# A decoder trunk with expert retrieval: one background chain split into two paced chains, with own weight rings, kept queries, eleven row tiles and a shared last sum

## The chip, the cores and the metric

The program runs on one core of one Trainium2 chip. The metric is device time in microseconds (us) of one execution; a smaller number is better. Engines are named as the profile names them: PE (matrix multiply), PEld (its weight loads), DVE (vector), ACT (activation), POOL (here it issues the gathers) and SP (here it issues the other DMAs). Each works through its own instructions in the order in which they stand.

## The reference, cut to what matters

A sequence of 272 tokens (16 meta tokens and 256 inputs, 1024 wide, float32) passes two layers. Layer 0 is a Conformer convolution, layer 1 a differential attention with 8 heads. After each comes a retrieval of experts:

```
def chunk(xc):                                   # 128 tokens at a time
    q = (xc @ wq).reshape(PEER_CHUNK, PEER_HEADS, 2, PEER_HALF)
    s1 = jnp.einsum('chd,kd->chk', q[:, :, 0], sk1)
    s2 = jnp.einsum('chd,kd->chk', q[:, :, 1], sk2)
    v1, i1 = lax.top_k(s1, PEER_TOPK)
    v2, i2 = lax.top_k(s2, PEER_TOPK)
    ...                                          # best 16 of the 256 sums v1 + v2
    expert = jnp.take_along_axis(cand_i, top_pos, axis=-1)
    gate = jax.nn.softmax(top_s.astype(jnp.float32), axis=-1).astype(xc.dtype)
    u = u_tab[expert]
    v = v_tab[expert]
    act = jax.nn.gelu(jnp.einsum('cd,chkd->chk', xc, u), approximate=False)
    return jnp.einsum('chk,chkd->cd', gate * act, v)
```

Each token reads 8 heads x 16 experts in each layer, and one expert is 1024 + 1024 floats (u and v side by side, 8 KB). A last rmsnorm gives the output, 256 x 1024.

## The kernel before, in words

**Row tiles and phases.** One gather (`Group.fetch`, L647) brings, for one head and one of its 16 choices, the expert of each of 128 tokens: a tile `row` of 128 x 2048 floats, 1 MB. I call this a row tile; there are 528, numbered from 0. They come in five phases (layer, token block): (0,0) is row tiles 0 to 127, the meta tokens (0,2) 128 to 143, (0,1) 144 to 271, (1,0) 272 to 399 and (1,1) 400 to 527. Each head of a phase is 16 row tiles in a row.

**What is done with one.** DVE multiplies its u half with the token vectors and sums (`product`, L653). For two row tiles together ACT takes the gelu (`gelu`, L658) and DVE multiplies by the gates (`weigh`, L662). For each row tile ACT then builds a diagonal matrix (L679) and PE adds the weighted v half to the sums in PSUM (`add`, L681: two matmuls, each of which the trace counts as two instructions). The row tile's buffer is free after that add. There are `NR = 10` buffers, so POOL can issue a gather only when the add ten row tiles earlier is done.

**The front.** Before the first gather stand the convolution and the choice of the first head. PE multiplies 16 blocks of `pw1` in three passes (`mm24`, L190); after block 0 stands the rmsnorm of the input (`stat`, L223, and `spread_rows`, L233).

**The background.** All other work is one generator, `background()`: the rest of the convolution, the choice of experts for layer 0, attention of token block 0, choice of (1,0), attention of block 1, choice of (1,1). The loop over row tiles pulls `RATE` units (0.3 to 1.2) of it for each row tile. The choice for one head is two queries (`query`, 8 matmuls L239 each), their scores (`ranked`, L555) with `top16` on DVE (L454 to L458), and `candidates`, `resolve` and `gates` (L508 to L539). For heads 2 to 7 of layer 0 one query serves both token blocks (272 columns), and both blocks are chosen at once (`for i in range(n)` in `ranked`). The recording layer then orders the instructions of each engine anew by its own estimates, so the program text is not the order on an engine.

**Weights.** Every 512 KB block of `fwq`, `wkvq` and `wo` passes through one ring of `NW = 5` buffers, in the one order of need, issued by SP (L165).

**The end.** After the last `add`, `final(1)` squares both halves on ACT (L863), takes the inverse root (`rsqrt`, with an ACT table load at L199), multiplies on DVE (L870) and writes two halves out from SP (L872).

## Time and profile before

| what | value |
|---|---|
| median of 3 runs | 1667.83 us (1666.53 to 1667.98) |
| the profiled execution | 1667.95 us |
| its span, first to last instruction | 1666.2 us |
| around the span | 1.75 us |
| read from HBM over the span | 627.51 MB, 377 GB/s |
| mean granted PE clock | 0.976 |

The profiled execution stands 0.12 us from the median. Busy times of the engines overlap and do not add up; a stage is read by what ends last in it.

### The profile page before, as it was taken

To read this page: it belongs to the slowest core of one execution; us is meant where nothing else is said; L and a number is where in the kernel's file an instruction comes from. 1 tells how busy PE (TensorE), PEld (TensorE's weight loads), DVE (VectorE), ACT (ScalarE), POOL (GpSimd) and SP (SyncE) were. 2 spreads that over 40 slices of the span, in tenths; PEclk is the share of its full clock that TensorE was granted. 3 is DMA by queue.
4 is the path that set the end of the run, shared out by engine and by line. 5 is a ranking of instruction groups with operands and counts; after the bars stand their busy time and mean duration, and the time that the engine had idled before them with its cause. 6 is when DMAs were issued, how large, how long until landed. Compare 5 with 4: busy or idle time off the path is not lost.

```text
span 1666.2 us, 18716 instructions
## 1 busy us (share of the span) xinstructions
PE 1441.8 (87%) x5560; PEld 828.2 (50%) x5560; DVE 1126.5 (68%) x3331; ACT 612.4 (37%) x1602; POOL 502.4 (30%) x533
## 2 busy tenths in 40 slices
PE   7998989988778799999888889999988787777776
PEld 7998745553222356656553356666553332223222
DVE  6984689998555465656996566666997555555554
ACT  8725434444112343453433254353342231121122
POOL 0001323333333323233224323232324343333330
PEclk9998999998999899999999999999999999999999
DMA  7301999998999999999999999999999999999996
GB/s 287 129 2 62 420 414 389 372 386 330 421 421 422 421 419 415 418 405 418 418 419 417 421 416 416 418 418 418 419 413 353 421 422 420 422 422 421 422 421 251
DMA packets 98388, 629.80 MB, mean 378 GB/s; under 512 B 11248, under 2 KB 11888, under 8 KB 30704
## 3 DMA queue, kind: packets, MB, share of 16 engines
q0 software_dynamic: 76032, 553.68, 80.8%
q1 hardware_dynamic: 22256, 74.92, 11.5%
q8 instruction: 46, 0.75, 0.2%
q14 instruction: 54, 0.44, 0.1%
HBM read 627.51 MB, written 1.05 MB: 377 GB/s over the span
## 4 chain that ended last, share of the span: by engine, by line
PE 35%; DMA 31%; DVE 29%; ACT 2%; issue 2%; POOL 0%; DVEq 0%; SPq 0%; POOLq 0%; ACTq 0%
DMA row<-in_fuv,eidx 29%; PE acc L681 21%; DVE row L653 10%; PE mm L239 7%; DVE vcc L394 3%; DVE scr L456 2%; PE mm L307 2%; DMA row<-in_fuv,meidx 1%; DVE oh L525 1%; DVE oh L528 1%; DVE ev L530 1%; DVE idxu L455 1%; DVE idxu L458 1%; DVE lo L143 1%; DVE pu L455 1%
## 5 line engine op out<-in xcount | busy, mean ns | idle before, releaser
L681 PE MATMUL acc<-row,dg 128*128 128x512 f32 x2048 | 963.1, 612 | 172.5 <-ACT dg L679 172.2
L647 POOL DMA_INDIRECT row<-in_fuv,eidx x512 | 485.4, 948 | 1107.3 <-PE acc L681 591.9
L653 DVE SCALAR_TENSOR_TENSOR row<-row,xps 128x1024 f32<-128x1024 f32 x528 | 639.8, 1215 | 249.3 <-DMA row<-in_fuv,eidx 233.4
L681 PEld LDWEIGHTS acc<-row,dg 128*128 128x128 f32 x2048 | 374.0, 193 | 640.5 <-issue 360.3
L658 ACT ACTIVATE dot<-dot,stf 128x2 f32<-128x2 f32 x256 | 75.6, 295 | 626.5 <-DVE row L653 626.1
L679 ACT ACTIVATE dg<-cst,dot 128x128 f32<-128x128 f32 x512 | 179.0, 394 | 157.7 <-DVE dot L662 148.4
L239 PEld LDWEIGHTS mm<-xin,w 128*128 128x128 f32 x1472 | 196.3, 194 | 39.2 <-issue 31.1
L239 PE MATMUL mm<-xin,w 128*128 128x128 f32 (+2 forms) x1472 | 214.2, 297 | 0.0
L662 DVE TENSOR_TENSOR dot<-dot,gate 128x2 f32<-128x2 f32 x256 | 40.8, 159 | 77.1 <-ACT dot L658 77.0
L658 ACT ACT_TABLE_LOAD x59 | 75.7, 1283 | 1.0
L394 DVE SCALAR_TENSOR_TENSOR vcc<-u,dw,vcc 128x272 f32<-128x272 f32 (+2 forms) x176 | 64.9, 412 | 0.6
L653 DVE DVE_READ_ACCUMULATOR row<-row,xps 128x1 f32 x528 | 43.3, 82 | 0.0
L537 ACT ACT_TABLE_LOAD x33 | 42.3, 1283 | 0.6
L714 DVE LOAD_MASK_SELECT rt<-mm x32 | 0.4, 14 | 56.0 <-PE mm L239 56.0
L555 PE MATMUL mm<-sk,qsb 128*128 128x128 f32 x120 | 24.3, 299 | 13.2 <-ACT qsb L547 13.2
L681 PE MATMUL acc<-row,mg 128*16 128x512 f32 x64 | 28.7, 593 | 7.6 <-ACT mg L675 7.6
L454 DVE MAX8 vals<-mm 128x8 f32<-128x128 f32 x64 | 18.5, 290 | 24.0 <-PE mm L555 23.8
L239 PEld LDWEIGHTS mm<-osb,w 128*128 128x128 f32 x256 | 30.9, 192 | 6.8 <-issue 5.5
L555 PEld LDWEIGHTS mm<-sk,qsb 128*128 128x128 f32 x120 | 18.7, 189 | 30.2 <-ACT qsb L547 21.2
L383 PE MATMUL acc<-u,dg 128*128 128x272 f32 x140 | 32.9, 392 | 0.0
L547 ACT ACTIVATE qsb<-mm 128x128 f32<-128x128 f32 (+2 forms) x48 | 14.6, 303 | 45.4 <-PE mm L239 44.9
L190 PE MATMUL mm<-xh,hi 128*128 128x272 f32 x128 | 24.8, 315 | 7.4 <-ACT hi L142 5.8
(222 smaller groups left out, 1226.5 us busy)
## 6 DMA issues: line engine op xcount, KB each, us to landing
w<-in_fwq SPq DMA_DIRECT2D x48, 512.0 KB, 8.4
w<-in_wkvq SPq DMA_DIRECT2D x48, 512.0 KB, 8.0
row<-in_fuv,eidx POOLq DMA_INDIRECT x512, 15.7
w<-in_wo SPq DMA_DIRECT2D x16, 512.0 KB, 8.7
raw<-in_pw SPq DMA_DIRECT2D x15, 512.0 KB, 4.0
row<-in_pw SPq DMA_DIRECT2D x8, 512.0 KB, 8.3
hT<-in_h SPq DMA_DIRECT2D x4, 272.0 KB, 5.0
out_dram<-row SPq DMA_DIRECT2D x4, 256.0 KB, 2.1
```

Source lines behind the costliest of these rows:

```text
L239: PE.matmul(out, lhsT=w[:, j, :], rhs=x[:, j, c0:c0 + n], start=(j == 0), stop=(j == ND - 1))
L307: PE.matmul(acc[:, :n], lhsT=pw2[b][:, d, :], rhs=cc[:, d, c0:c0 + n], start=(d == 0 and not part), stop=(d == ND - 1))
L394: V.scalar_tensor_tensor(out=y, in0=x, scalar=dw[:, i, k:k + 1], in1=y, op0=ALU.mult, op1=ALU.add)
L455: V.max_index(out=idx[:, 0:8], in_max=vals[:, 0:8], in_values=src)
L537: S.activation(g, g, AF.Exp, scale=rts, accum_out=sm)
L555: PE.matmul(sc[:, i * P:(i + 1) * P], lhsT=q[:, i * P:(i + 1) * P], rhs=sk[:, layer, half, :], start=True, stop=True)
L647: GP.indirect_dma_start(out=r, out_offset=None, in_=a["fuv%d" % self.layer], in_offset=bass.IndirectOffsetOnAxis(ap=self.e[:, k:k + 1], ax ...
L653: V.scalar_tensor_tensor(out=u, in0=u, scalar=1.0, in1=self.ph.xps, op0=ALU.mult, op1=ALU.mult, accum_out=self.dot[:, k:k + 1])
L658: S.activation(d, d, AF.Gelu, scale=self.ph.rt)
L662: V.tensor_tensor(out=d, in0=d, in1=self.g[:, k:k + SUB], op=ALU.mult)
L679: S.activation(g, ident, AF.Copy, scale=w)
L681: PE.matmul(out[half], lhsT=g, rhs=r[:, half * 512:(half + 1) * 512], start=first, stop=last, skip_group_check=self.layer == 1)
```

## The change

The one background generator becomes two: `selection()` (all choices of experts) and `attending()` (both attentions and the first output), each pulled at its own constant pace in all phases: `SELECT` is 1.0 units for each of the first 32 row tiles and 0.55 after them, `ATTEND` 0.68. Each has its own weight ring: `wq` with 5 buffers and `wa` with 3, both still issued by SP. For layer 0 a query of 272 columns now chooses token block 0 alone; the columns of block 1 are kept in `qlate` (12 buffers) and chosen later by `choose_late`. The input of layer 1's choice gets its own buffer `xnext`. There are 11 row tiles instead of 10; the buffer `sg` moves into free columns of `vcc` for it. In the front, the rmsnorm of the input stands after block 1 of `pw1` instead of block 0. At the end the last two row tiles are taken one by one, the last one's second half is added by DVE (L703) instead of PE, and `close()` shares the last norm among ACT and DVE and writes the halves from SP and ACT.

```
-NR = 10
-NW = 5
+NR = 11
+NQ = 5
+NA = 3
-RATE = {(0, 0): 1.15, (0, 1): 1.1, (1, 0): 1.2, (1, 1): 0.3}
+SELECT = (1.0, 0.55)
+ATTEND = 0.68
...
-    weights = Weights([a["fwq"][0, j] for j in range(16)] + per_half + per_half)
+    queries = Weights("wq", NQ, [a["fwq"][l, j] for l in (0, 1, 1) for j in range(16)])
+    shared = Weights("wa", NA, ([a["wkvq"][j] for j in range(24)] + [a["wo"][j] for j in range(8)]) * 2)
...
-            cb(b, acc)
+            if b:
+                if b == 1:
+                    cb(0, before)
+                cb(b, acc)
+            before = acc
...
-            q = wk.tile([P, T], F32, name="qsb")[:, 0:n]
-            S.activation(q, acc[:, :n], AF.Copy)
+            q = wk.tile([P, P], F32, name="qsb")
+            S.activation(q, acc[:, off:off + P], AF.Copy)
+            if n == T:
+                late[h, half] = wk.tile([P, P], F32, name="qlate", bufs=12)
+                S.activation(late[h, half], acc[:, M + P:T], AF.Copy)
...
+        def choose_late(h):
+            vals = wk.tile([P, 1, 2, M], F32, name="vals")
+            idxu = wk.tile([P, 1, 2, M], U32, name="idxu")
+            for half in range(2):
+                yield from ranked(0, half, late.pop((h, half)), 1, vals, idxu)
+            yield from picked(0, h, [1], vals, idxu, rts0)
...
+                closing = (self.layer, self.t, self.h) == (1, 1, 7)
+                if closing and last:
+                    preload(AF.Sqrt)
+                    y = wk.tile([P, 512], F32, name="qhalf", bufs=1)
+                    V.scalar_tensor_tensor(out=y, in0=r[:, 512:1024], scalar=w, in1=out[1], op0=ALU.mult, op1=ALU.add)
+                    box["half"] = y
...
+        def close():
+            src = [phases[1, 1].acc[0], box["half"]]
+            gr = [box["grow"][:, k * 512:(k + 1) * 512] for k in range(2)]
+            ss = wk.tile([P, 2], F32, name="fss", bufs=1)
+            z = rp.tile([P, 2 * D], F32, name="row")
+            V.scalar_tensor_tensor(out=z[:, D:D + 512], in0=src[1], scalar=1.0, in1=src[1], op0=ALU.mult,
+                                   op1=ALU.mult, accum_out=ss[:, 1:2])
+            S.activation(z[:, D + 512:], src[0], AF.Square, accum_out=ss[:, 0:1])
+            V.tensor_tensor(out=z[:, 512:1024], in0=src[1], in1=gr[1], op=ALU.mult)
+            s1 = wk.tile([P, 1], F32, name="fs1", bufs=1)
+            V.tensor_tensor(out=s1, in0=ss[:, 0:1], in1=ss[:, 1:2], op=ALU.add)
+            r = rsqrt(wk, s1, 1, 1.0 / D, tag="f",
+                      meanwhile=lambda: V.tensor_tensor(out=z[:, 0:512], in0=src[0], in1=gr[0], op=ALU.mult))
+            V.tensor_scalar(out=z[:, 512:1024], in0=z[:, 512:1024], scalar1=r, scalar2=None, op0=ALU.mult)
+            S.activation(z[:, 0:512], z[:, 0:512], AF.Copy, scale=r)
+            for k in range(2):
+                (SY, S)[k].dma_start(out=out_ap[P:2 * P, k * 512:(k + 1) * 512], in_=z[:, k * 512:(k + 1) * 512])
...
+            yield from early(2)
+            yield from choose_late(0)
+            yield from early(3)
+            yield from early(4)
+            yield from choose_late(1)
+            yield from early(5)
+            yield from early(6)
+            yield from early(7)
...
+            yield from choose_meta()
+            for h in range(2, 8):
+                yield from choose_late(h)
+            for t in range(2):
+                yield from until(t)
+                yield from ready_layer1(t)
...
+                select.run(SELECT[0] if s < 2 * M else SELECT[1])
+                attend.run(ATTEND)
```

What the change does to the order on an engine is shown at three places. The first is PE in phase (0,0), near row tile 30: `xin,w` and `xin,wq` are queries of both token blocks, `sk,qsb` scores of a kept query, `row,dg` the adds. Before:

```order
L681 MATMUL acc<-row,dg 128x512 x8
L239 MATMUL mm<-xin,w 128x272 x5
L555 MATMUL mm<-sk,qsb 128x128 x2
L239 MATMUL mm<-xin,w 128x272 x4
L681 MATMUL acc<-row,dg 128x512 x4
L239 MATMUL mm<-xin,w 128x272 x4
L555 MATMUL mm<-sk,qsb 128x128 x2
```

And in the changed kernel:

```order
L241 MATMUL mm<-xin,wq 128x272 x5
L565 MATMUL mm<-sk,qsb 128x128
L241 MATMUL mm<-xin,wq 128x272
L707 MATMUL acc<-row,dg 128x512 x4
L241 MATMUL mm<-xin,wq 128x272 x4
L707 MATMUL acc<-row,dg 128x512 x4
```

Behind each query now stands one block's scores instead of two, and the next query follows sooner: the twelve queries of heads 2 to 7 stand between the adds of row tiles 13 and 52, before between 11 and 60.

The second place is SP in the front, where `raw` are blocks of `pw1` and `w`, `wq`, `wa` ring blocks. Before, from the loads of `pw2` (`row<-in_pw`) on:

```order
L420 DMA row<-in_pw 128x1024 x8
L135 DMA raw<-in_pw 128x1024 x3
L469 DMA sk<-in_sk 128x256 x2
L165 DMA w<-in_fwq 128x1024
L476 DMA mask<-in_cst 128x128
L477 DMA rope<-in_cst 128x544
```

In the changed kernel:

```order
L427 DMA row<-in_pw 128x1024 x8
L137 DMA raw<-in_pw 128x1024 x3
L167 DMA wq<-in_fwq 128x1024
L167 DMA wa<-in_wkvq 128x1024
L137 DMA raw<-in_pw 128x1024 x2
L167 DMA wa<-in_wkvq 128x1024 x2
L137 DMA raw<-in_pw 128x1024 x3
```

Three attention blocks now load in the front; before, the first of them stood behind eleven more `fwq` blocks that wait for buffers.

The third place is the end of DVE, after the weighing of the last row tiles. Before:

```order
L662 TENSOR_TENSOR dot<-dot,gate 128x2
L865 TENSOR_TENSOR fs_10194<-fss 128x1
L198 TENSOR_SCALAR rs_vf<-fs_10194 128x1
L202 RECIPROCAL rs_rf<-rs_sf 128x1
L203 TENSOR_TENSOR rs_sf<-rs_rf 128x1
L204 SCALAR_TENSOR_TENSOR rs_sf<-rs_sf,rs_vf 128x1
L205 SCALAR_TENSOR_TENSOR rs_rf<-rs_sf,rs_rf 128x1
L870 SCALAR_TENSOR_TENSOR row<-acc,rs_rf,zk 128x512 x2
```

In the changed kernel:

```order
L681 TENSOR_TENSOR dot<-dot,gate 128x1
L703 SCALAR_TENSOR_TENSOR qhalf<-row,dot,acc 128x512
L905 SCALAR_TENSOR_TENSOR row,fss<-qhalf 128x512
L908 TENSOR_TENSOR row<-qhalf,zk 128x512
L910 TENSOR_TENSOR fs_10239<-fss 128x1
L912 TENSOR_TENSOR row<-acc,zk 128x512
L198 TENSOR_SCALAR rs_vf<-fs_10239 128x1
L204 RECIPROCAL rs_rf<-rs_sf 128x1
L205 TENSOR_TENSOR rs_sf<-rs_rf 128x1
L206 SCALAR_TENSOR_TENSOR rs_sf<-rs_sf,rs_vf 128x1
L207 SCALAR_TENSOR_TENSOR rs_rf<-rs_sf,rs_rf 128x1
L913 TENSOR_SCALAR row<-row,rs_rf 128x512
```

Four wide instructions moved in ahead of the root, and one multiplication by it (L913) remains behind it.

## Rows read from the trace of the kernel before

**Rows 1.** The page: 40 equal slices of the span, DMA share and rate.

```profile
DMA  7301999998999999999999999999999999999996
GB/s 287 129 2 62 420 414 389 372 386 330 421 421 422 421 419 415 418 405 418 418 419 417 421 416 416 418 418 418 419 413 353 421 422 420 422 422 421 422 421 251
```

**Rows 2.** Windows by stage: length, each engine busy (instructions), PE clock, DMA share, GB/s.

```profile
0.00:158.00 158.00, 143.42 (x974) 135.49 (x974) 124.41 (x390) 94.62 (x239) 2.01 (x5) 0.96 0.31 110
158.00:240.00 82.00, 76.67 (x372) 53.99 (x373) 54.56 (x189) 35.30 (x92) 28.25 (x30) 0.94 0.99 407
240.00:410.00 170.00, 155.26 (x467) 83.67 (x466) 163.75 (x626) 75.42 (x165) 55.50 (x58) 0.96 0.95 369
410.00:1240.00 830.00, 745.48 (x3030) 425.30 (x3029) 551.02 (x1647) 310.97 (x837) 267.68 (x283) 0.99 1.01 418
1240.00:1290.00 50.00, 42.93 (x111) 19.81 (x110) 38.46 (x104) 16.43 (x40) 20.21 (x22) 0.93 0.92 360
1290.00:1640.00 350.00, 263.49 (x580) 104.47 (x579) 184.12 (x358) 73.80 (x218) 128.73 (x138) 0.99 1.01 421
1640.00:1666.00 26.00, 14.54 (x32) 5.49 (x31) 10.15 (x23) 5.90 (x15) 0.00 (x0) 0.91 0.37 151
```

**Rows 3.** Waits of POOL between 240 and 410 us: total us, times, longest.

```profile
POOL row L647 <- PE acc L681: 67.3, 28, 7.0
```

**Rows 4.** DVE's products (L653) alone in stretches; each row tile counts two instructions.

```profile
205.00:329.60 124.60, 45.93 (x76) 0.97 0.99 394
329.60:394.25 64.65, 24.28 (x40) 0.90 0.90 350
1156.58:1259.10 102.52, 38.93 (x64) 1.00 1.00 405
```

**Rows 5.** All engines, 240.3 to 394.25 us, columns as in Rows 2.

```profile
240.30:394.25 153.95, 139.21 (x430) 76.40 (x430) 150.17 (x597) 69.40 (x150) 47.65 (x49) 0.95 0.94 370
```

**Rows 6.** DVE by line, 240.3 to 394.2 us: count, busy, mean ns, idle before.

```profile
L653 DVE SCALAR_TENSOR_TENSOR row<-row,xps 128x1024 f32<-128x1024 f32 x48 | 57.7, 1203 | 0.0
...
L530 DVE TENSOR_REDUCE ev<-oh 128x32 f32<-128x512 f32 x13 | 8.8, 673 | 0.0
```

**Rows 7.** Chain that ended last, 183 to 220 us: start, us, what.

```profile
206.95 3.67 PE mm L239 x16
...
212.33 0.45 PE mm L555 x4
212.78 3.44 PE acc L681 x8
```

**Rows 8.** All engines in block 1's attention, columns as in Rows 2.

```profile
1002.00:1127.00 125.00, 125.00 (x632) 81.43 (x631) 80.06 (x239) 58.38 (x163) 37.93 (x40) 1.00 1.02 417
```

**Rows 9.** The page's DMA issues: KB each, median us to landing.

```profile
w<-in_wo SPq DMA_DIRECT2D x16, 512.0 KB, 8.7
```

**Rows 10.** The same by tile w: landing, shortest, median, longest.

```profile
DMA to landing us min/median/max: 4.5/8.2/14.3
```

**Rows 11.** Timeline of PE, 12 to 19 us: start, us, what, idle before.

```profile
13.92 2.06 PE L223 MATMUL mm<-one,sa 128*128 128x1 f32 x18
18.32 1.12 PE L233 MATMUL mm<-cst,stc 16*128 16x16 f32 x3 [2.33 <-DVE stc L227]
```

**Rows 12.** Timeline of the end, columns as in Rows 11.

```profile
1652.33 1.22 DVE L653 SCALAR_TENSOR_TENSOR row<-row,xps 128x1024 f32<-128x1024 f32 x1 [1.25 <-DMA row<-in_fuv,eidx]
...
1657.51 0.60 ACT L863 ACTIVATE row<-acc 128x512 f32<-128x512 f32 x1 [2.64 <-PE acc L681]
...
1659.07 1.28 ACT L199 ACT_TABLE_LOAD   x1
...
1660.37 0.20 ACT L199 ACTIVATE rs_sf<-rs_vf 128x1 f32<-128x1 f32 x1
...
1661.46 1.41 DVE L870 SCALAR_TENSOR_TENSOR row<-acc,rs_rf,zk 128x512 f32<-128x512 f32 x2
1662.24 0.99 SPq L872 DMA_DIRECT2D out_dram<-row  x2
```

More of the change, by code (lines that the diff above doesn't have):

```diff
@@ L201, in rsqrt @@
             preload(then)
+        if meanwhile is not None:
+            meanwhile()
         V.reciprocal(out=r, in_=s)
@@ L421, in conv @@
                     pw2.append(w)
-                for _ in range(NW - 1):
-                    weights.fetch()
+                for _ in range(NQ - 1):
+                    queries.fetch()
         for i in range(ND - LAG, ND):
@@ L679, in add @@
                     S.activation(g, ident, AF.Copy, scale=w)
-                for half in range(2):
-                    PE.matmul(out[half], lhsT=g, rhs=r[:, half * 512:(half + 1) * 512], start=first, stop=last,
+                closing = (self.layer, self.t, self.h) == (1, 1, 7)
[4 more added lines that the diff above has]
+                    box["half"] = y
+                for half in range(1 if closing and last else 2):
+                    stop = last or (closing and half == 1 and k == M - 2)
+                    PE.matmul(out[half], lhsT=g, rhs=r[:, half * 512:(half + 1) * 512], start=first, stop=stop,
                               skip_group_check=self.layer == 1)
@@ L774, in attention @@
                 acc = bank()
-                mm8(acc[:, :P], weights.get(), xb, 0, P)
+                mm8(acc[:, :P], shared.get(), xb, 0, P)
                 qT = wk.tile([P, P], F32, name="qT")
@@ L797, in attention @@
                 yield
-                w = weights.get()
+                w = shared.get()
                 acc = bank()
@@ L851, in ready_layer1 @@
             ph.src = (xq, 0)
-            yield
             for h in range(8):
-                yield from choose(1, h, xq, n, [t], 0, [ph.rt])
+                yield from choose(1, h, xq, n, t, 0, [ph.rt])
         def final(t):
             c0, n = cols(t)
-            src = phases[1, t].acc if t else [phases[1, t].row[:, k * 512:(k + 1) * 512] for k in range(2)]
+            src = [phases[1, t].row[:, k * 512:(k + 1) * 512] for k in range(2)]
             ss = wk.tile([P, 2], F32, name="fss", bufs=1)
@@ L889, in trunk @@
         xa = xq0[:, :, 0:n]
-        first = [[weights.get(), weights.get()] for _ in range(2)]
+        first = [[queries.get(), queries.get()] for _ in range(2)]
         fill = box["fill"]
@@ L896, in trunk @@
                 next(ln)
-        one = choose(0, 0, xa, n, [0], M, rts0, first[0])
+        one = choose(0, 0, xa, n, 0, M, rts0, first[0])
         for _ in range(5):
@@ L907, in trunk, with until, selection @@
             pass
-        def background():
+        attended = {}
+        def until(t):
+            while t not in attended:
+                yield True
+        def selection():
             for b, _ in enumerate(point(1, lambda b: gain(1, b))):
@@ L912, in background @@
                     yield
-            yield from choose(0, 1, xa, n, [0], M, rts0, first[1])
+            yield from choose(0, 1, xa, n, 0, M, rts0, first[1])
             take(1)
@@ L961, in background, with __init__, run @@
             yield from final(0)
+        class Paced:
+            def __init__(self, units):
+                self.units, self.credit, self.left = units, 0.0, True
+            def run(self, rate):
+                self.credit += rate
+                while self.left and self.credit >= 1.0:
+                    self.credit -= 1.0
+                    said = next(self.units, 0)
+                    self.left = said != 0
+                    if said:
+                        self.credit = 0.0
+        select, attend = Paced(selection()), Paced(attending())
         order = [(0, 0, h) for h in range(8)]
-        bg = background()
         order.insert(META_AT, (0, 2, 0))
         order += [(l, t, h) for l, t in ((0, 1), (1, 0), (1, 1)) for h in range(8)]
-        credit, left, slots = 0.0, True, []
+        slots = []
         total = M * len(order)
@@ L973, in trunk @@
                     while key not in chosen:
-                        assert not next(bg), key
+                        if next(select.units):
+                            assert not next(attend.units), key
                     cur = Group(*key)
@@ L995, in trunk @@
                 g.add(k)
-            if s % SUB == SUB - 1 and s < total:
+            if s % SUB == SUB - 1 and s < total - SUB:
                 cur.gelu(s % M - SUB + 1)
-        for _ in bg:
-            pass
-        for _ in final(1):
-            pass
+        assert not next(select.units, 0) and not next(attend.units, 0)
+        close()
         st.close()
```

87 lines of the change are left out of this document (35 added, 52 removed).

## Prediction

> **What bounds the kernel now.** I read the page's forty slices first [rows 1]: from the fifth slice on the DMA rate stands at 413 to 422 GB/s almost everywhere, and the places where it does not are few. So I cut the span into stages at those places [rows 2]. The best long stage, 1290 to 1640 us, moves 421 GB/s for 350 us; I take that as the rate of a full DMA. At it a row tile (1.0486 MB) costs 2.49 us and a weight block (0.5243 MB) 1.245 us, and the 629.8 MB of the whole execution (627.5 read from HBM, 1.05 written, the rest instructions) 1496 us. What remains of the 1666.2 us, 170 us, is time in which DMA is not full. Stage by stage it is length x (421 - rate) / 421: 116.7 us before the first gathers, 2.7 to 240 us, **21.0** from 240 to 410, **5.9** from 410 to 1240, **7.2** from 1240 to 1290, none to 1640, and 16.7 at the end. The change leaves the bytes alone (112 weight blocks and 528 row tiles before and after), so every microsecond must come out of one of these gaps.
>
> Why is DMA not full from 240 to 410 us? POOL's longest wait there is 67.3 us in 28 waits for an add on PE, that is for a free row buffer [rows 3]: all ten are full. Behind it stands DVE, busy 150.17 of 153.95 us, 97.5% [rows 5], with choices of experts between its products. Between 205 and 394.25 us it does products 13 to 71 in two pieces, 39 in 124.6 us at 394 GB/s and 20 in 64.65 us at 350 [rows 4]: gaps of 8.0 and 10.9 us of the 21.0. The gap at 1250 us has the same cause: the eight choices of (1,1) beside 32 products in 102.5 us [rows 4].
>
> **The change part by part.**
>
> *The choices in phase (0,0).* One choice for one head and one block costs DVE: 150.17 less 48 products (57.7 us) and 24 weighings (about 0.16 us each, an estimate from DVE's other instructions, 3.8), over 13 choices [rows 5, 6], so 6.8 us. A product with its share of weighing is 1.28 us. By the order, the changed DVE finishes 7 choices between products 13 and 52 (before 9), and 5 between 52 and 72 (meta among them; before also 5). That makes 7 x 6.8 + 39 x 1.28 = 97.5 us and 5 x 6.8 + 20 x 1.28 = 59.6 us.
>
> But the order on PE moves too: the twelve wide queries now stand between adds 13 and 52. A query is 3.67 us, a score 0.22, two adds 3.44 [rows 7]: 12 x 3.67 + 16 x 0.22 + 39 x 1.72 = 114.6 us. DMA needs 39 x 2.49 = 97.1 us and about 14 of the sixteen `wq` blocks, 17.4: 114.5 us. So this piece is no longer DVE's but PE's and DMA's in equal parts. I divide by the 97.5% that the bounding engine reached: 118 us, against 124.6, a gain of 6.6 us. It can't be under 114.5 (gain 10); the low end is 0, if PE waits as DVE did. In the second piece DVE has as many choices as before: they are hoisted to where they were, and 64.65 us stay. I take a gain of 1.0 (DVE arrives there with less backlog), between 0 and 13.5 (what remains of the 21.0 gap).
>
> *The eleventh row tile* lets DVE fall behind by one more row tile before DMA runs dry: 2.5 us here. Together 10.1 of the 21.0 us. Zero is its low end; more than 2.49 a buffer can't give at one place.
>
> *Own rings.* SP now loads three `wa` blocks in the front, where DMA is nearly idle (110 GB/s, [rows 2]); they were loaded in the full stretch before. Gain 3 x 1.245 = **3.7 us**, from 0 (if they delayed `raw`, which has idle DMA around it) to 3.7.
>
> *The last choices, (1,1).* By the order the eight choices stand between products 366 and 398, again 32 row tiles, with the same eleven blocks. I expect the same knot some 45 us later, 2.5 us shorter by the eleventh buffer: gain **2.5** of 7.2. DVE holds its choices a little closer together there than before, so the low end is a loss of 5; the high end is 7.2.
>
> *The two chains in between.* 410 to 1240 us loses 5.9 us in all. Attention of block 0 stands between adds 146 and 214 (before 145 to 203), attention of block 1 between 276 and 362 (before 274 to 328), now with choices of (1,0) between its parts. PE gets fewer products a row tile than in the old stretch, which already ran at 417 GB/s with PE busy 125 of 125 us [rows 8]. I take **0**, bounds -16 (below) and +5.9. Twelve more copies of kept queries on ACT lie in time in which ACT is busy 75.42 of 170 us [rows 2]; uncovered they would be 12 x 0.3, 3.6 us.
>
> *The front.* With the norm behind block 1, PE no longer idles 2.33 us ahead of `spread_rows` for want of other work [rows 11], but it will idle there one block later. DVE's long row of taps starts when the first `u` is there, and block 1 is by then done. Gain **1.0**, between 0 and 2.3.
>
> *The end.* Before, the last product ends at 1653.55 and the span 12.65 us later [rows 12]. After it I count, from those rows: gelu and weighing to 0.53, diagonal to 1.0, table load 1.28, its dummy 0.2, square 0.6 and its readout 0.2 to 3.15; the sum of squares 0.2; then DVE's L912 (0.70, half of the 1.41 pair), which stands ahead of L198 in the order, to 4.1; four-step root with its ACT part 1.3, to 5.4; the last multiplication 0.75, to 6.15; then the 3.3 us that lay between the old last multiplication (1662.87) and the end. 9.5 us against 12.65: gain **3.2**, from 1.8 to 4.0.
>
> The count rests on a table load of 1.28 us, and the next ACT instruction begins 1.30 us after the load began [rows 12]. The Trainium skill, page "ScalarE: Activation LUTs", section "What ACT_TABLE_LOAD costs", says that a switch costs the load and a drain of about 1.38 us more, 2.66 us in all. By the page the square would come 1.4 us later and the end would gain 1.8, and the sum below would be 1648.9; I go by the row, where no drain shows.
>
> **Sum.** 10.1 + 3.7 + 2.5 + 0 + 1.0 + 3.2 = 20.5 us. From the profiled execution's 1667.95 us (1.75 more than its span, 0.12 from the median of 1667.83): **1647.5 us**.
>
> **The rivals.**
>
> *PE takes DVE's place in full.* If PE, with 114.6 us of work and waits for ACT and DVE in between, needs the old 124.6 us, 6.6 us are lost: **1654 us**. For it: three engines have 97 to 115 us of work in the same stretch. Against it: DVE alone bounded at 97.5%, and two others ran beside it. Chance 0.20.
>
> *The knots vanish.* If the eleventh buffer and the looser order cover both knots, the remaining 10.9 and 4.7 us go as well: **1632 us**. For it: the mean load fits DMA's. Against it: products 52 to 72 still ask 59.6 us of DVE for 49.8 us of row tiles. Chance 0.12.
>
> *Three buffers are too few for `wo`.* These eight blocks stand 1.25 row tiles apart by the order, about 4.4 us at DMA's rate. A block is asked for when the third before it is used up, so it has about 8.7 us to land. The median is 8.7, the longest landing of any block 14.3 [rows 9, 10]. At the median nothing is lost; if all came like the longest, each of 2 x 8 blocks would cost up to 1 us, the rings elsewhere too: 16 us, **1663 us**; more likely some 8, 1655. Chance 0.10.
>
> *The two chains get in each other's way, and it is slower.* From adds 274 to 350, PE's own order mixes attention and choices, four PSUM banks serve both, and a product that waits holds up all adds behind it. By the order there are 35 eight-part products of 128 columns (1.73 us each, 3.67 x 128/272) and 76 adds: 191 us, 2.5 a row tile; before 32 in 54 adds, 2.75. DMA needs (76 x 2.49 + 35 x 1.245) / 76 = 3.06. PE's scores and transposes and all its waits must therefore pass 0.55 a row tile to cost anything, and reach 0.83 to eat the 20.5 us. At 1.0 a row tile it is 1647.5 + 76 x 0.45 = **1682 us**. For it: nothing in the old trace has two chains. Against it: the denser stretch of [rows 8]. Chance 0.07.
>
> *The reordering undoes it.* Choices are hoisted so far forward that the knots stay as they were, and only front, rings and end remain: 1667.95 - 7.9 = **1660 us**. For it: the second piece. Against it: 7 choices instead of 9 in the first, by the order. Chance 0.08.
>
> **How the numbers follow.** The forecast has 0.43, its own range 1642 to 1652 (first piece 3 to 10, second 0 to 3, the others near their values). The range that leaves out 2 in 10 runs from just above the vanished knots to the reordering that undoes it: **1634 to 1660 us**. A measurement of this kernel tells about 0.2%, 3.3 us, from no change. All cases but the two chains and the worst of the late weights lie below 1661; I give faster 0.90, same 0.03, slower 0.07.
>
> **What would show it right or wrong.** The rate from 240 to 410 us should rise from 369 to about 395 GB/s, and DVE's share from products 13 to 52 fall below 90% while PE's comes near full; the front should move about 1.6 MB more. The dip at 1250 us should stand near 1280 to 1310 and be shallower. The span should end about 9.5 us after the last product. The forecast is wrong if a new dip appears between 750 and 800 us or between 900 and 1200 us (waits of PE for `wa`, or of POOL for adds), or if the old dip keeps its 21 us.

## The result and the profile after

The changed kernel takes **1695.4 us** (median of 4 runs, 1691.3 to 1696.5) against 1667.9 before: ratio 1.016, 95% interval 1.0141 to 1.0179. It is 27.5 us slower, where 20 us faster was forecast. The profiled execution took 1695.23 us with a span of 1692.9.

The windows by stage of the changed kernel (columns as in [rows 2]):

```profile
0.00:158.00 158.00, 143.47 (x974) 135.49 (x974) 125.70 (x391) 94.65 (x239) 2.04 (x6) 0.96 0.34 120
158.00:240.00 82.00, 81.12 (x393) 57.63 (x394) 51.58 (x173) 35.44 (x98) 29.75 (x32) 0.97 0.99 408
240.00:320.00 80.00, 76.75 (x249) 44.32 (x247) 71.45 (x258) 33.20 (x84) 24.78 (x26) 1.00 1.01 415
320.00:410.00 90.00, 74.35 (x190) 35.41 (x191) 78.47 (x278) 33.08 (x76) 31.10 (x33) 0.91 0.90 342
410.00:600.00 190.00, 149.25 (x390) 60.27 (x388) 118.95 (x315) 53.00 (x146) 68.75 (x73) 0.96 1.01 421
...
900.00:1200.00 300.00, 266.18 (x1089) 154.49 (x1088) 199.51 (x622) 114.19 (x294) 91.67 (x97) 0.97 1.00 411
1200.00:1400.00 200.00, 180.02 (x746) 107.91 (x745) 151.01 (x512) 80.74 (x197) 62.94 (x66) 0.97 0.95 375
1400.00:1692.90 292.90, 213.12 (x462) 82.77 (x460) 152.20 (x296) 59.85 (x178) 99.56 (x106) 0.99 0.97 403
```

The last column is the one to read. With the prediction's measure, length x (421 - rate) / 421, each window gives the time in which DMA was not full. The table does this for the kernel before, the changed one and, since all comparisons below use it, for the experiments (one profiled execution each; medians and ratios are of all timed runs). The windows are cut by time, so in a slower kernel the same work stands somewhat further on; the rate is rounded to 1 GB/s, which is up to 0.7 us in a window of 300 us.

| kernel | median us | ratio (interval) | 0-240 | 240-320 | 320-410 | 410-600 | 600-900 | 900-1200 | 1200-1400 | 1400-end |
|---|---|---|---|---|---|---|---|---|---|---|
| before | 1667.9 | | 119.4 | 7.2 | 13.9 | 0.0 | 3.6 | 2.1 | 7.1 | 16.4 |
| **changed** | 1695.4 | 1.016 | 115.5 | 1.1 | 16.9 | 0.0 | **22.1** | **7.1** | **21.9** | 12.5 |
| e1 one chain | 1666.0 | 0.9989 (0.998-0.9999) | 116.7 | 1.3 | 19.9 | 1.8 | 1.4 | 5.0 | 8.6 | 13.2 |
| e2 ten rows | 1702.0 | 1.021 (1.0193-1.0227) | 116.5 | 3.0 | 16.9 | 3.2 | 20.7 | 9.3 | 21.4 | 12.8 |
| e3 even rings | 1690.9 | 1.0136 (1.0119-1.0153) | 115.1 | 1.3 | 17.1 | 2.3 | 18.9 | 8.6 | 17.6 | 12.3 |
| e4 attend faster | 1673.5 | 1.0043 (1.0027-1.006) | 115.5 | 1.1 | 17.7 | 0.0 | 19.6 | 1.4 | 6.2 | 13.5 |
| e5 order kept | 1733.1 | 1.039 (1.037-1.041) | 115.9 | 7.0 | 13.0 | 29.3 | 19.6 | 5.0 | 15.7 | 28.2 |
| e6 choices kept | 1726.8 | 1.0344 (1.032-1.0367) | 115.1 | 7.2 | 11.8 | 27.1 | 19.6 | 2.9 | 14.7 | 33.5 |
| e7 before, kept | 1712.6 | 1.0263 (1.0236-1.0291) | 119.8 | 11.6 | 12.8 | 6.3 | 12.1 | 10.0 | 27.1 | 15.5 |
| e8 kept, even rings | 1733.0 | 1.0387 (1.0364-1.041) | 116.5 | 7.2 | 12.6 | 29.3 | 20.0 | 5.0 | 16.6 | 26.7 |
| e9 paces by phase | 1677.7 | 1.0055 (1.0035-1.0074) | 115.3 | 1.3 | 17.1 | 2.7 | 6.1 | 14.3 | 12.4 | 13.2 |
| e10 choices slow | 1660.3 | 0.9966 (0.9952-0.9979) | 115.3 | 1.1 | 17.3 | 0.0 | 7.5 | 1.4 | 5.7 | 14.1 |
| e11 paces, even rings | 1673.5 | 1.0026 (1.0013-1.0038) | 115.3 | 1.1 | 17.3 | 5.4 | 5.7 | 8.6 | 9.5 | 13.6 |
| e12 late choices held | 1665.6 | 0.9985 (0.9976-0.9995) | 115.9 | 0.2 | 0.2 | 8.1 | 9.0 | 11.4 | 10.9 | 13.2 |
| **e13 slow and held** | 1647.7 | 0.9876 (0.986-0.9893) | 115.9 | 0.2 | 0.0 | 4.1 | 7.1 | 1.4 | 5.7 | 13.9 |
| e14 held, 0.8 | 1648.4 | 0.9875 (0.9858-0.9891) | 117.1 | 0.2 | 3.8 | 0.0 | 1.5 | 5.7 | 10.0 | 12.9 |
| e15 held, 1.0 | 1649.7 | 0.9884 (0.9868-0.9901) | 115.3 | 0.4 | 3.8 | 4.5 | 3.6 | 1.4 | 10.0 | 13.6 |
| e16 attend slower | 1693.2 | 1.0145 (1.0128-1.0162) | 117.3 | 0.4 | 16.7 | 0.5 | 18.2 | 9.3 | 22.3 | 13.2 |
| e17 second faster | 1672.7 | 1.0034 (1.0021-1.0047) | 115.3 | 1.0 | 17.1 | 5.0 | 7.1 | 9.3 | 10.5 | 14.4 |
| **e18 held, even rings** | 1646.9 | 0.9877 (0.986-0.9893) | 116.5 | 0.2 | 0.0 | 4.1 | 6.1 | 1.4 | 4.3 | 15.1 |

So the front, the first piece and the end gained (3.9, 6.1 and 3.9 us). Lost were 3.0 in the second piece and, above all, 18.5 from 600 to 900 us, 5.0 to 1200 (the second attention) and 14.8 from 1200 to 1400, where the choices of (1,1) stand.

The 18.5 us fall in three parts of similar size. Before and in the changed kernel:

```profile
600.00:740.00 140.00, 135.81 (x634) 85.43 (x633) 85.88 (x264) 65.97 (x191) 40.33 (x44) 1.00 1.02 417
740.00:800.00 60.00, 58.72 (x307) 40.22 (x306) 37.93 (x131) 20.75 (x57) 17.78 (x19) 1.00 1.01 410
800.00:900.00 100.00, 88.32 (x334) 49.42 (x332) 92.31 (x319) 39.97 (x92) 35.20 (x36) 0.98 1.01 417
```

```profile
600.00:740.00 140.00, 132.52 (x593) 80.84 (x594) 81.48 (x247) 56.50 (x165) 40.38 (x43) 1.00 1.00 401
740.00:800.00 60.00, 51.94 (x224) 31.31 (x223) 29.53 (x78) 22.18 (x66) 16.91 (x18) 0.94 0.94 374
800.00:900.00 100.00, 84.68 (x261) 42.77 (x260) 64.67 (x178) 29.76 (x76) 34.79 (x38) 0.95 0.95 384
```

The heads of the first attention, to 740 us, lose 6.7 where 1.3 were lost before; the end of the last head and most output products, to 800, 6.7 (before 1.6); the first two choices of (1,0), which stand behind them by themselves, 8.8 (before, with all eight, 1.0).

**Where the heads lose.** One head in the changed kernel, PE's timeline (start, us, what, and idle before it with its releaser):

```profile
643.96 0.52 PE L811 MATMUL mm<-zk,qT 64*128 64x144 f32 x4
644.41 2.23 PE L241 MATMUL mm<-xin,wa 128*128 128x144 f32 x16
647.08 0.33 PE L831 MATMUL mm<-cst,vt 128*128 128x128 f32 x1 [0.44 <-DMA row<-in_fuv,eidx]
...
647.36 3.70 PE L707 MATMUL acc<-row,dg 128*128 128x512 f32 x8
651.07 0.33 PE L848 MATMUL mm<-cst,e 128*128 128x128 f32 x1
...
651.88 0.49 PE L855 MATMUL mm<-vcc,at 128*128 128x128 f32 x2 [0.37 <-ACT at L850]
...
652.71 3.34 PE L241 MATMUL mm<-xin,wa 128*128 128x144 f32 x26
655.89 3.65 PE L707 MATMUL acc<-row,dg 128*128 128x512 f32 x8
659.38 0.83 PE L241 MATMUL mm<-xin,wa 128*128 128x128 f32 x6
660.04 3.60 PE L707 MATMUL acc<-row,dg 128*128 128x512 f32 x8
663.57 0.52 PE L811 MATMUL mm<-zk,qT 64*128 64x144 f32 x4
```

And in e10, whose attention there is pulled at 1.1 units a row tile:

```profile
650.27 0.52 PE L811 MATMUL mm<-zk,qT 64*128 64x144 f32 x4
650.72 1.98 PE L707 MATMUL acc<-row,dg 128*128 128x512 f32 x4
652.54 2.12 PE L241 MATMUL mm<-xin,wa 128*128 128x144 f32 x16
654.50 1.02 PE L707 MATMUL acc<-row,dg 128*128 128x512 f32 x2
655.36 0.27 PE L831 MATMUL mm<-cst,vt 128*128 128x128 f32 x1
...
655.58 1.02 PE L707 MATMUL acc<-row,dg 128*128 128x512 f32 x2
656.44 0.27 PE L848 MATMUL mm<-cst,e 128*128 128x128 f32 x1
...
656.65 1.88 PE L707 MATMUL acc<-row,dg 128*128 128x512 f32 x4
658.37 0.39 PE L855 MATMUL mm<-vcc,at 128*128 128x128 f32 x2
...
668.20 0.52 PE L811 MATMUL mm<-zk,qT 64*128 64x144 f32 x4
```

In both a head has three weight blocks and the adds of six row tiles (a row tile shows as x4). DMA needs 6 x 2.49 + 3 x 1.245 = 18.7 us for it. e10 takes 17.9, the changed kernel 19.6: PE is the bound, with the same work. The reader is to see where the adds stand: in e10 one row tile lies between a step of the head and the next, which needs the first one's answer from ACT or DVE; in the changed kernel the adds come two row tiles at a time (x8), steps stand side by side, and PE waits 0.44 and 0.37 us a head. The remaining 0.9 us shows in no idle time; it is in longer steps from one start to the next. e4's heads from 702 us on (0.9 units) have their adds as x8 and x16 and take 20.0 us: the loss goes with the pattern.

**Where the stretch behind the heads loses.** PE in the changed kernel:

```profile
754.60 9.85 PE L707 MATMUL acc<-row,dg 128*128 128x512 f32 x16 [4.04 <-ACT dg L698]
...
785.77 1.35 PE L241 MATMUL mm<-osb,wa 128*128 128x128 f32 x10 [2.43 <-DMA wa<-in_wo]
...
829.36 10.02 PE L707 MATMUL acc<-row,dg 128*128 128x512 f32 x16 [1.98 <-ACT dg L698]
...
856.24 32.56 PE L707 MATMUL acc<-row,dg 128*128 128x512 f32 x72 [5.39 <-ACT dg L698]
```

At 754 us PE has no product left to do while ACT loads two tables, for a gelu and for the norm of the attention, 1.28 us each, ahead of the next `dg`. At 786 it waits for a block of `wo`. At 829 and 856 DVE chooses, and PE waits for a `dg` with nothing else to do. From 740 to 860 us the kernel before has no wait of PE for `dg` above 1.1 us, and none for weights.

**Where the last choices lose.** PE at the border of the phases, row tile 400, and one window there:

```profile
1339.72 7.38 PE L707 MATMUL acc<-row,dg 128*128 128x512 f32 x16
1352.55 9.54 PE L707 MATMUL acc<-row,dg 128*128 128x512 f32 x16 [5.46 <-ACT dg L698]
1362.78 3.70 PE L707 MATMUL acc<-row,dg 128*128 128x512 f32 x8 [0.69 <-ACT dg L698]
1366.32 1.04 PE L634 MATMUL xps<-cst,xnext 128*128 128x128 f32 x8
```

```profile
1350.00:1360.00 10.00, 7.45 (x12) 3.32 (x13) 9.88 (x34) 4.65 (x9) 1.07 (x1) 0.66 0.48 192
```

DVE is busy 9.88 of 10 us with choices and products, so PE idles 5.46 us for its next `dg`. It then works off four row tiles in 9.54 us, the same that took 7.38 us ahead of the idle time, at a granted clock of 0.66. At that point the phase ends: the new phase's input must be transposed (`xps`, behind the adds), and DVE's next product waits for it:

```profile
1367.39 1.22 DVE L672 SCALAR_TENSOR_TENSOR row<-row,xps 128x1024 f32<-128x1024 f32 x1 [2.36 <-PE xps L634]
...
1370.83 0.69 DVE L651 COPY row<-acc 128x512 f32<-128x512 f32 x1 [2.21 <-PE acc L707]
```

**The end.** From the last product on, the changed kernel:

```profile
1682.93 0.08 DVE L672 DVE_READ_ACCUMULATOR row<-row,xps 128x1 f32 x1
...
1684.06 1.28 ACT L126 ACT_TABLE_LOAD   x1
...
1685.35 0.20 ACT L126 ACTIVATE scrap<-one 128x1 f32<-128x1 f32 x1
```

From the end of that product, 1683.01, to the span's end 9.9 us go by, against 12.65 in [rows 12].

### The profile page after: what moved, and what is told of

Its sections match the earlier page's. It is cut to its first block, busy times and chain, and to the rows that moved or that the text cites. A ratio compares the mean times of both kernels' runs of the same rounds, so it can differ in the third digit from the quotient of the medians.

```text
span 1692.9 us, 18686 instructions
## 1 busy us (share of the span) xinstructions
PE 1453.4 (86%) x5558; PEld 833.2 (49%) x5558; DVE 1124.5 (66%) x3336; ACT 612.6 (36%) x1614; POOL 502.7 (30%) x533
## 3 DMA queue, kind: packets, MB, share of 16 engines
q1 hardware_dynamic: 22112, 74.66, 11.4%
## 4 chain that ended last, share of the span: by engine, by line
PE 40%; DMA 27%; DVE 27%; ACT 3%; issue 2%; POOL 0%; SPq 0%; POOLq 0%; ACTq 0%; DVEq 0%
DMA row<-in_fuv,eidx 25%; PE acc L707 25%; DVE row L672 8%; PE mm L241 8%; DVE vcc L397 3%; DMA wa<-in_wo 2%; PE mm L310 2%; DVE scr L463 1%; DVE oh L532 1%; DVE oh L535 1%; DVE ev L537 1%; DVE idxu L465 1%; PE mm L190 1%; DVE idxu L462 1%; DVE pu L465 1%
## 5 line engine op out<-in xcount | busy, mean ns | idle before, releaser
L677 ACT ACTIVATE dot<-dot,stf 128x2 f32<-128x2 f32 (+1 forms) x257 | 75.8, 295 | 606.9 <-DVE row L672 604.5
L681 DVE TENSOR_TENSOR dot<-dot,gate 128x2 f32<-128x2 f32 (+1 forms) x257 | 40.8, 159 | 77.9 <-ACT dot L677 73.5
L241 PEld LDWEIGHTS mm<-xin,wa 128*128 128x128 f32 x640 | 80.6, 193 | 12.1 <-issue 9.3
L241 PE MATMUL mm<-xin,wa 128*128 128x128 f32 (+1 forms) x640 | 85.4, 285 | 0.0
L241 PEld LDWEIGHTS mm<-xnext,wq 128*128 128x128 f32 x512 | 62.3, 192 | 8.2 <-issue 7.9
L241 PE MATMUL mm<-xnext,wq 128*128 128x128 f32 x512 | 65.4, 276 | 0.0
L241 PE MATMUL mm<-xin,wq 128*128 128x272 f32 (+2 forms) x320 | 64.0, 348 | 0.0
L241 PEld LDWEIGHTS mm<-xin,wq 128*128 128x128 f32 x320 | 51.6, 190 | 13.9 <-issue 8.1
L461 DVE MAX8 vals<-mm 128x8 f32<-128x128 f32 x64 | 18.7, 294 | 55.9 <-PE mm L565 55.7
L554 ACT ACTIVATE qsb<-mm 128x128 f32<-128x128 f32 x48 | 13.2, 274 | 77.7 <-PE mm L241 75.1
L241 PE MATMUL mm<-osb,wa 128*128 128x128 f32 x256 | 33.2, 284 | 6.3 <-DMA wa<-in_wo 5.5
```

Of the source, the lines that this page charges most:

```text
L241: PE.matmul(out, lhsT=w[:, j, :], rhs=x[:, j, c0:c0 + n], start=(j == 0), stop=(j == ND - 1))
L461: V.max(out=vals[:, 0:8], in_=src)
L677: S.activation(d, d, AF.Gelu, scale=self.ph.rt)
L681: V.tensor_tensor(out=d, in0=d, in1=self.g[:, k:k + n], op=ALU.mult)
```

## The experiments

The first theory was that two chains side by side cost by themselves; rivals were the short attention ring and the eleventh row tile.

**e1**: choices and attention in one chain again.

```diff
-SELECT = (1.0, 0.55)
-ATTEND = 0.68
+RATE = {(0, 0): 1.15, (0, 1): 1.1, (1, 0): 1.2, (1, 1): 0.3}
...
-            for t in range(2):
-                yield from until(t)
-                yield from ready_layer1(t)
+            yield from attending()
...
-            attended[0] = True
+            yield from ready_layer1(0)
```

> The changed kernel with choices and attention again in one chain, pulled at the old rates of the four phases; rings, kept queries, eleven row tiles, front and end stay. If the two chains side by side are what costs (theory A), the losses between 600 and 900 us (22 us, before 4), between 1000 and 1300 us and at the choices of (1,1) (17 us, before 7) go back to those of before, and what is left of the gains is the front (4.8 us) and the end (1.6): 1658 to 1664 us. If the split ring is what costs (theory B: 3 buffers starve attention, 5 lie idle beside it), the rings are the same here and the time stays above 1680 us.

1666.0 us. The middle is healed (600 to 900: 1.4), so the rings and the kept queries are not what costs there. It came out above the range because 240 to 410 us loses 21.2, as before: up to row tile 72 its choices stand as in the changed kernel, and three more follow up to row tile 79.

**e2** (`NR = 10`) and **e3** (`NQ = 4`, `NA = 4`):

> The changed kernel with 10 row tiles instead of 11; the order of instructions is the same. If the eleventh buffer is worth a row tile at each knot, as the prediction had it (2.5 us, and there are now about five knots), 1700 to 1708 us. If the knots are longer than what one buffer covers and the buffer only shifts where they begin, 1695 to 1698 us.

1702.0: the buffer is worth 6.6 us in all, near the low end of what was expected; 1.9 of it lie in the first piece, and nothing at the last choices.

> The changed kernel with 4 buffers in each ring instead of 5 and 3, same order. Theory B (the attention ring is too short): the stretch 600 to 800 us, which now loses 13 us, loses half of it or less, and the time is 1685 to 1690 us. Theory A: PE waits for a wa block only 2.7 us in all between 600 and 800 us, so at most 3 us are to be had: 1692 to 1698 us.

1690.9, 4.5 less: the ring is too short by a little, in the stretches that lose most; it is not the main cause.

**e4**: `ATTEND = 0.9`.

> The changed kernel with attention pulled at 0.9 units a row tile instead of 0.68. By the order the second attention ends at row tile 331 instead of 350 and the eight choices of (1,1) stand at 355 to 379 instead of 373 to 397, as dense as before but away from the border of the phases at row tile 400. If that border (the result rows of phase (1,0), its norm and its output, which hold row buffers and PE) is what makes this knot deeper than before's, its loss falls from 17 to about 8 us: 1684 to 1689 us. If density alone makes it (eight choices in 25 row tiles instead of 29), it stays: 1693 to 1699 us.

1673.5, 22 us less from one constant, and below both ranges. Moved off the border, the choices of (1,1) lose 6.2 with the stretch around them instead of 21.9, and the second attention, which the expectation left out, 1.4 instead of 7.1. The stretch of the first attention, 600 to 900, stays at 19.6. **e16** (`ATTEND = 0.62`) asked the other way round:

> The changed kernel with attention at 0.62 units a row tile instead of 0.68. By the order the eight choices of (1,1) stand at row tiles 383 to 409, as dense as in the changed kernel (373 to 397) and with the border of the phases at 400 in their midst. If the border makes the knot deep, it loses 15 us or more again, and the time stays at 1690 us or above. If it is something else that the faster attention took away, the knot is near 6 us.

1693.2, and 1200 to 1400 loses 22.3 (13.6 of it from 1300 to 1400, where 15 or more was expected; the rest ahead of it). In all runs but those with the kept order (e5 to e8, below), 1200 to 1400 loses 18 to 22 us where the eight choices reach row tile 397 or beyond (the changed kernel, e2, e3, e16) and 4 to 12 where they end by row tile 379 (the others): the border it is. What spreads the others from 4 to 12 no run shows: the choices of e9 (12.4) and e10 (5.7) stand two row tiles apart.

**e5 to e8** tried the thought that the reordering undoes what the two chains deal out. The code writes the choices of (1,1) at row tiles 389 to 478; they are issued at 373 to 397.

```diff
         for j in range(ND):
-            PE.matmul(out, lhsT=w[:, j, :], rhs=x[:, j, c0:c0 + n], start=(j == 0), stop=(j == ND - 1))
+            i = PE.matmul(out, lhsT=w[:, j, :], rhs=x[:, j, c0:c0 + n], start=(j == 0), stop=(j == ND - 1))
+            if j == 0 and box.get("dealt"):
+                tc.keep_in_program_order(i)
```

(and the same for the scores; e6 for queries and scores of choices alone; e7 in the kernel before; e8 with `NQ = 4`, `NA = 4`).

> The changed kernel, with the first matmul of every query, key, value, output product and score issued on PE behind all that is written ahead of it. It only fixes the order in which instructions are issued: the choices of (1,1), written at row tiles 389 to 478, are issued on DVE at 373 to 397 in the changed kernel and at 385 to 474 here; the heads of the first attention at 159 to 220 (7.6 row tiles a head) instead of 155 to 199 (6). Theory H (the instructions are issued far ahead of where the two chains deal them, and the heaps cost): the knot of 17 us at 1350 us goes, 600 to 900 us loses under 10 instead of 22, 240 to 410 us under 10 instead of 18: 1645 to 1660 us. Theory A (two chains cost by themselves on in-order engines, whatever the order): 1685 us or more.

> As the run with the whole order kept, but only queries and scores of the choices are kept in the written order; attention may be issued ahead again (first attention at 159 to 203, 6 row tiles a head). Under theory H the knot at 1350 us is gone here too, and the stretch 600 to 750 us loses the 7 us that it loses in the changed kernel, so 4 to 7 us above the run with the whole order kept. If attention's place is of no matter, the two agree within 2 us.

> The kernel before, with the same two places kept in the written order: its choices in (0,0) and after then stand at row tiles 23 to 91 instead of 22 to 73, those of (1,1) at 339 to 379 instead of 339 to 368. If issuing ahead is what makes the knots of before too (theory H), 240 to 410 us loses 10 to 14 instead of 21 and the knot at 1250 us 3 instead of 7.5: 1652 to 1659 us. If the order is only of matter with two chains, 1666 to 1669 us.

> As the run with the whole order kept, with 4 buffers in each weight ring instead of 5 and 3. With rings alone the changed kernel gained 4 us, in the output products of attention (around 800 us) and at the second norm (around 1250 us). If those waits for weights are there with the kept order too, 3 to 5 us below the run with the whole order kept; if they came from the heaps, no difference beyond 1.5 us.

1733.1, 1726.8, 1712.6 and 1733.0 us: this theory fell, all four were slower, the kernel before by 44 us. With the order kept, even rings change nothing. Spread out, most lone choices make a dip of their own: in e5, 10 of the 15 that end between 417 and 625 us and between 1370 and 1600 us, of 2 us or more each. One of them in e5, PE's timeline and ACT's:

```profile
1525.35 10.55 PE L711 MATMUL acc<-row,dg 128*128 128x512 f32 x20 [4.07 <-ACT dg L702]
1535.74 1.95 PE L241 MATMUL mm<-xnext,wq 128*128 128x128 f32 x16
```

```profile
1537.72 0.28 ACT L556 ACTIVATE qsb<-mm 128x128 f32<-128x128 f32 x1 [6.47 <-PE mm L241]
1537.90 0.29 ACT L681 ACTIVATE dot<-dot,stf 128x2 f32<-128x2 f32 x1
```

While DVE chooses, PE has nothing else to do and idles 4.07 us. Then the next query waits behind 20 adds; ACT waits 6.47 us for that query's copy, with the gelu of the next products behind it. Three queues wait for each other in turn. The two lone choices of (1,0) in the changed kernel, at 829 and 856 us above, look the same. That queries issued far ahead help because they fill PE and leave ACT free is my reading; no run parts the two.

**e9** gave each phase paces of its own, **e10** slow choices throughout:

```diff
-SELECT = (1.0, 0.55)
-ATTEND = 0.68
+SELECT = (1.0, 0.55, 1.1, 0.55, 0.55)
+ATTEND = (0.68, 0.68, 1.1, 0.9, 0.68)
...
-                select.run(SELECT[0] if s < 2 * M else SELECT[1])
-                attend.run(ATTEND)
+                stage = 0 if s < 2 * M else 1 + sum(s >= M * x for x in (9, 17, 25))
+                select.run(SELECT[stage])
+                attend.run(ATTEND[stage])
```

(e10: 0.55 in the third place of `SELECT`.)

> The changed kernel with two chains and both rings as they are, but with paces by phase: choices 1.0 and 0.55 up to the meta tokens as now, then 1.1 in (0,1); attention 1.1 in (0,1) and 0.9 in (1,0). By the order (0,0) is as in the changed kernel; the heads of the first attention stand 5.4 row tiles apart (6 in the changed kernel), the choices of (1,0) at 214 to 241, those of (1,1) at 353 to 377. Theory P (the slow constant pace costs, not that there are two chains): 600 to 900 us loses 2 to 5 instead of 22, the second attention and the last choices together about 8 as with the faster attention, 240 to 410 us stays near 18: 1653 to 1661 us. If chains or rings cost by themselves, 600 to 900 us stays near 20: 1668 to 1674 us.

> As the run with paces by phase, but the choices keep 0.55 in (0,1): five of (1,0) at 215 to 230, three at 283 to 311 amid the second attention. It parts theory P: the attention's pace made the losses of 600 to 800 us, the choices' pace those of 830 to 870 us (9 of the 22). If so, 7 to 11 us above the run with paces by phase; if attention's pace made all of it, within 3 us of it.

In e9 the stretch of the first attention is healed (6.1), with two chains and the same rings, and with choices at 0.55 as in the changed kernel it stays so (e10, 7.5): attention's pace was the cause. In e10 all three parts shrink: the heads lose 2.0, the stretch to 800 us 1.0, the choices behind it 4.5 (1.2 in e9, with the choices at 1.1). But e9's second attention loses 14.3, which I had not expected, and the whole is 1677.7 (its runs lie between 1671.1 and 1681.9). e10 was to be slower than e9 and is 17 us faster: three choices beside the second attention, at the same pace, take its loss to 1.4. **e11** (e9 with `NQ = 4`, `NA = 4`) and **e17** (1.1 in the fourth place of both):

> As the run with paces by phase, with 4 buffers in each weight ring instead of 5 and 3. In the changed kernel this gained 4 us. If that was weights that come late whatever the pace, 3 to 4 us below the run with paces by phase; if it came from the heaps, within 1.5 us of it.

> As the run with paces by phase (1677.7 us), with both chains at 1.1 units a row tile in (1,0) too instead of 0.55 and 0.9. No choice stands beside the second attention in either; its heads stand 5.7 row tiles apart instead of 6.7, the choices of (1,1) at 344 to 372 instead of 353 to 377. If attention alone loses time where less than about one unit of it falls on a row tile, 900 to 1200 us loses 3 to 5 instead of 14 and the time is 1665 to 1670 us. If it loses because no other chain runs beside it, 14 us stay: 1675 us or more.

1673.5: 4.2 us for the rings again, with intervals that just overlap. 1672.7: the faster second attention loses 9.3, between what the two theories said; it settles nothing.

**e12 to e15** and **e18**: the choices of block 1 (kept queries) held on DVE alone.

```diff
-    def top16(src, vals, idx, scr):
-        V.max(out=vals[:, 0:8], in_=src)
+    def top16(src, vals, idx, scr, pin=False):
+        first = V.max(out=vals[:, 0:8], in_=src)
+        if pin:
+            tc.keep_in_program_order(first)
```

(`pin` in `choose_late` only; e12 on e9; e13 on e10; e14 and e15 on e10 with 0.8 and 1.0 in the second place of `SELECT`; e18 is e13 with `NQ = 4`, `NA = 4`.)

> As the run with paces by phase; in layer 0 the choices of block 1 (kept queries) start on DVE behind all products that are written ahead of them, so five of them go from the heap of row tiles 57 to 71 to row tiles 115 to 154. PE and ACT are not held. If the heap on DVE makes the dip of 320 to 410 us (17 us there), it falls to about 9 and the choices further on cost nothing, as DVE has room there: 6 to 9 us below the run with paces by phase. If a lone choice costs 3 to 4 us wherever it stands, as in the run with the whole order kept, the dip shrinks and five dips come up between 500 and 620 us: 4 to 15 us above it.

> The run with paces by phase and slow choices (0.55 throughout, 1660.3 us), with the choices of block 1 in layer 0 held on DVE behind what is written ahead of them: they stand 9 to 10 row tiles apart, at 115 to 162. If the stages are independent, its losses are those of the slow choices (7.9 us from 600 to 900, 7.2 from 1000 to 1300) and those of the held ones (0.6 from 240 to 410, 8.3 from 410 to 600): 10 us below, 1648 to 1652 us. If the gain of the one undoes the other, 1658 us or more.

> As the run before in this list, with choices at 0.8 units a row tile after the first 32: the held choices stand 6 to 7 row tiles apart, at 90 to 122. If a lone choice costs about 1.6 us wherever it stands, the time is the same within 2 us. If choices close together share their price, the 8 us between 410 and 600 us fall to about 4: 1644 to 1648 us. If density is all (6.8 us of DVE against 1.2 us to spare in a row tile, so 5.6 row tiles a choice), they cost nothing here or at 10 apart.

> As the run before in this list, with 1.0 units a row tile: the held choices stand 5 row tiles apart, at 79 to 104, closer than the 5.6 at which DVE keeps up. By density six choices ask 73 us of DVE in 62 us of row tiles, 11 too many, of which the eleven row buffers cover a part: 410 to 600 us loses up to 8 us. If choices close together share their price, 2 to 4 us and a time at or below that of the run at 0.8.

> The fastest run so far (slow choices, late ones held, 1647.7 us) with 4 buffers in each weight ring instead of 5 and 3. The even rings gained 4 us in the changed kernel and 4 us with paces by phase, in stretches that lost 11 to 22 us. If the weights of the attention ring come late whatever the pace, 1643 to 1645 us. If the rings only matter where attention goes in heaps, which it doesn't here, 1646.5 to 1649 us.

e12: 320 to 410 us falls from 17.1 to 0.2 and 410 to 600 rises from 2.7 to 8.1; 12 us less than e9 in all. (By the order three choices moved away, not five: eight instead of eleven now stand between row tiles 26 and 72. At 6.8 us each that is 20 us less for DVE, against 17 of loss. They are missing from the first piece, not from the five close together at row tiles 57 to 71, which stand in both: in e9 four choices stand at 37 to 48, in e12 none between 35 and 57.) e13: 1647.7, the two gains add up. Its windows over that stretch:

```profile
240.00:320.00 80.00, 77.83 (x229) 41.50 (x228) 66.24 (x217) 26.20 (x73) 29.19 (x31) 1.00 1.01 420
320.00:410.00 90.00, 81.01 (x238) 40.94 (x236) 74.03 (x236) 33.25 (x83) 31.61 (x34) 0.98 1.01 421
410.00:600.00 190.00, 149.45 (x424) 63.40 (x424) 137.13 (x417) 63.22 (x166) 65.35 (x69) 0.94 1.00 412
```

e14 and e15 agree with e13 within 2 us: what is saved where the held choices stand (4.1 in e13, 0.0 and 4.5) is paid elsewhere (3.8 at the second piece and 10.0 from 1200 to 1400 instead of 0.0 and 5.7), so the price of distance stays open. e18: 1646.9, no difference; the rings matter only where attention goes in heaps. e13 and e18 beat both kernels: 1.2% below before, 2.8% below the changed kernel.

## Why the prediction was wrong, step by step

**Right:** the front (4.7 forecast; 3.9 from 0 to 240, and the first product comes 1.1 us earlier). The first piece of (0,0), in kind: from 240 to 320 us PE is busy 96% and DVE 89%, as it said. From the product of row tile 14 to that of row tile 52 it now takes 119.8 us (206.56 to 326.33) instead of 124.5 (205.84 to 330.31): 4.7 gained of 6.6 forecast. The sum there counts 39 products where [rows 4] show 38; with 38 PE would have 112.9 us of work, and by the same reckoning the gain would have been 8.8. The end: 9.5 us after the last product forecast, 9.9 measured, so 2.8 gained of 3.2; why the whole stage gained 3.9 no run takes apart. The table load at the end cost its row's time: the next ACT instruction begins 1.29 us after it. The Trainium skill ("ScalarE: Activation LUTs", "What ACT_TABLE_LOAD costs") would have 1.38 us more; no run here shows them.

**The eleventh row tile** is worth 6.6 us (e2), but not where the sum had it: 1.9 instead of 2.5 in the first piece, and nothing instead of 2.5 at the last choices.

**The second piece** was to gain 1.0 and lost 3.0. The prediction saw that as many choices stand there as before and left it. e12 has as many there too and loses nothing: with three choices fewer in the first piece the second one is no longer short, so its loss was a debt from the first, which the prediction had expected to shrink.

**"The two chains in between", taken as 0, is the step that failed most**: 23.5 us lost between 600 and 1200. It counted PE's products for each row tile, found fewer than before and concluded that PE had room. That mean says nothing on whether a row tile's adds lie between one step of a head and the next, nor on what PE has to do while ACT or DVE is taken. The first attention had no price at all: the two chains' rival was placed between adds 274 and 350, which lost 5 us, while 18.5 went to a stretch where each chain ran *alone*: 5.4 more than before in the heads, 5.1 from the last head through the output products, 7.8 at two choices behind them. That rival (1682 us, 0.07) had the right side and the wrong mechanism: where both chains run beside each other, little is lost at 0.9 units (e10, e4), and one slow chain by itself loses most. For 600 to 900 us the attention's pace is shown to be the cause (0.68 in the changed kernel, 0.9 in e4, 1.1 in e10, the choices at 0.55 in all: 22.1, 19.6 and 7.5); how it does so is read from the traces above, and no run takes the three parts apart. For the second attention, why it loses 14 alone at 0.9 and 1.4 with three choices beside it is not settled. The prediction had named new dips from 750 to 800 and from 900 to 1200 us as signs that it is wrong; both came.

**"The last choices", taken as +2.5, lost 14.8**, three times the low end. The prediction read their new place (row tiles 366 to 398) from the order and did not price that the phase ends at 400. e4 and e16 show that the place makes the difference, with choices as dense.

**Three buffers too few** cost some 4 us (e3), half of that rival's price, and nothing in e18. **The reordering undoes it** holds in part: it brings kept choices into the two pieces of (0,0), and holding DVE alone there is worth 12 us (e12 against e9, e13 against e10); but with PE held to the written order everything is slower (e5 to e8).

The sum of 1647.5 us was within reach of this design: e13 measures 1647.7, with attention's pace set by phase and the late choices held. That the two agree so closely is luck: against before, e13 gains 20.9 us from 240 to 410 where the sum had 10.1, and loses 6.9 from 410 to 1200 where it had nothing.

## What to carry to other kernels

A mean load of an engine per tile doesn't price a stretch with serial chains: look in the order at what stands between a step and the next one that needs its answer, and at what the engine has to do while it waits. When work is moved, look at what lies at its new place, above all where a phase ends and the pipeline drains. And before blaming a structure, turn its constants: one pace was worth 22 of the 27 us here, and an instruction held on one engine's queue did what holding the whole order spoiled.

## What was not expected of the hardware

An idle PE can pay twice. Behind the 5.46 us of idle time at the border, in steps of 2 us (columns as in [rows 2]):

```profile
1354.00:1356.00 2.00, 2.00 (x3) 0.67 (x2) 1.98 (x7) 0.30 (x1) 0.00 (x0) 0.50 0.46 193
1356.00:1358.00 2.00, 2.00 (x4) 0.86 (x3) 1.93 (x9) 1.84 (x3) 0.00 (x0) 0.64 0.04 8
1358.00:1360.00 2.00, 2.00 (x6) 0.95 (x5) 2.00 (x5) 1.82 (x4) 1.07 (x1) 1.00 0.00 0
```

The granted clock fell to 0.50, the lower of its two levels (1.2 and 2.4 GHz), and was back at 1.00 from 1358 us on; 16 adds took 9.54 us instead of 7.38. In e5, after 4.07 us, 20 adds took 10.55 us, 0.53 each, where 16 in 7.38 are 0.46. The price varies: after 5.39 us, at 856.24 us in the changed kernel, 72 adds took 32.56 us, 0.45 each. At the border the transfers stop for a while too: POOL issued no gather from 1348.80 to 1358.93 us, and the rate fell to 8 and 0 GB/s. Whether the slow adds or the products of DVE held the row buffers then is open, since the profile puts that wait down to a product that ended just then.
